# One more projection by seven half-size products, its input sums one group sooner, and three pieces of a decoder block's side work moved

## The chip, the cores and the metric

The kernel runs on one core of one Trainium2 chip. Its time is the device time of one execution in microseconds (us); a run's time is the median over executions. The engines are TensorE (PE, matrix products), VectorE (DVE), ScalarE (ACT), GpSimd (POOL), and SyncE (SP), which only issues transfers. Each takes its instructions in the order written.

## The reference

One layer of a decoder trunk, float32, 512 tokens, model width 1024:

```
h = RMSNorm(x);  h @ w_in -> GLA q, k, v, gate r, forget input
                             | attention q, k, v for 3 groups | two merge gates
A: gated linear attention, 4 heads, chunks of 64 (decay = exp of a running sum of log_sigmoid)
B: causal dilated attention, 3 groups x 4 heads, dilation 1, 4, 16; groups merged by softmax weight
x += (sigmoid(gA) * (A @ w_o_gla) + sigmoid(gB) * (B @ w_o_attn)) @ w_out
x += relu(RMSNorm(x) @ w_mlp1)^2 @ w_mlp2
x += sigmoid(RMSNorm(x) @ w_pg) * (p @ w_pp)
out = RMSNorm(x)
```

## The kernel before

Activations lie transposed (features on partitions, 512 tokens along the row). A product in float32 is made of three passes: each operand is split into a high part `hi` (rounded to fp32r, on ACT) and a rest `lo` (on DVE), and hi x hi, hi x lo, lo x hi are summed in PSUM. Weights come as units of 128 x 1024 (512 KB): `load` brings one to one of six raw buffers, and `fetch` makes its `hi` (line 226) and its `lo` (line 221). `weight` asks `fetch` to be two operands ahead of the one that PE is about to use. All matmuls of split products are recorded at line 240, in `run`.

There are two forms of a 1024 x 512 x 512 projection. The plain one (`fm`) is four units, each 24 matmuls with 512 columns. The other (`strassen`) takes 2 x 2 blocks of weights and inputs and does seven half-size products instead of eight, the rows of `STAGES`, each 24 matmuls with 256 columns. Its operands are blocks and sums of blocks of the weights: S1 and S3 are added up by an accumulating transfer that POOL issues (`prepare`, `sums`, lines 198 and 209), S2 and S4 by DVE (lines 206 and 212); the block A21 of a quad is loaded five operands early. The input sums T1 to T4 come from `xsums` and are split too. Results: a first product is copied from PSUM with ACT (line 312), and a later one is combined with it on DVE (line 330 or 332).

Everything else is side work, written as generators. `run` calls `step` after each eight matmuls; `step` takes one closure from the list `later` and, whenever `pace` columns have gone by, one piece of the first generator in `side`, which then goes back to second place (`WAYS` = 2). So two generators alternate, and a generator further down the list waits. `drain` runs all that is left without products between. The place of a piece in the program decides where it stands in each engine's queue.

The order: q0, k0 (group 0), a drain that ends with the normed input, then q1 and k1 (group 1, plain) with `scores0` and `xsums` as side work, a drain, q2 and k2 (seven products), v1 and v2 with `scores12`, v0, then gq, gk and gv0 with `pv` (attention output, one per head) and `decay` (the GLA decays, eight pieces with PE, then Exp, Ln and the scan on ACT and DVE), then the w_o_attn product with `gla` for two heads, the gates, w_o_gla, w_out, the MLP, w_pp, w_pg and the output. All intermediate 128 x 512 tiles come from one pool of `NU` tiles.

In the MLP, `rms_gen` makes 1/rms of the new x for each token: matmuls with ones, a power on POOL (`rsqrt`), a diagonal tile `dg`, its split, and two matmuls (lines 396, 397) that broadcast it. Each block of the hidden layer is `max(., 0) * rstd` (line 1167), then squared (line 1176). At the end, `evac_pg0` and `evac_pg1` take w_pg's result for 128 tokens: sigmoid (ACT, line 1267), two DVE operations, the square with its sum (ACT, line 1270), and then `scale_out` and `put` scale and store. The last 128 tokens are done in two halves of 256 columns.

Of the kernel before, what the change touches and what calls it, by code (L numbers as in the profile page):

```python
# [13 lines left out]
AF = mybir.ActivationFunctionType  # L14
OP = mybir.AluOpType
# [19 lines left out]
def att_col(g, which):  # L35
    return ATT + (g * 3 + which) * 512
# [5 lines left out]
def weight_units():  # L42

    u = []

    def fm(name, src, col, n, row=0):
        for j in range(n):
            u.append((f"{name}.{j}", "fm", src, row, col + j * P))

    def tm(name, src, col):  # L50
        for i in range(4):
            u.append((f"{name}.{i}", "tm", src, i * 2 * P, col))

    fm("q0", "w_in", att_col(0, 0), 4)
    u = u[NS:]
    def quad(name, src, col, kind="quad"):
        for m, k in ((0, 0), (1, 0), (1, 1), (0, 1)):
            u.append((f"{name}.A{m + 1}{k + 1}", kind, src, k, col + m * (P if kind == "quad" else 256)))

    fm("k0", "w_in", att_col(0, 1), 4)  # L60
    fm("q1", "w_in", att_col(1, 0), 4)
    fm("k1", "w_in", att_col(1, 1), 4)
    quad("q2", "w_in", att_col(2, 0))
    quad("k2", "w_in", att_col(2, 1))
    quad("v1", "w_in", att_col(1, 2), "quadt")
# [12 lines left out]
    for i in range(2):
        quad(f"ga{i}", "w_in", GATE + i * 512)
    fm("og", "w_o_gla", 0, 8)  # L80
    fm("wo", "w_out", 0, 8)
    for q in range(8):
        quad(f"m1q{q}", "w_mlp1", q * 512)
    for sub in range(2):
        for kk in range(16):
            u.append((f"m2s{sub}.{kk}", "tm", "w_mlp2", kk * 2 * P, sub * 512))
    for j in range(2):
        u.append((f"pp{j}.0", "tm", "w_pp", 0, j * 512))
    for j in range(2):
        tm(f"pg{j}", "w_pg", j * 512)  # L90
    return u
# [35 lines left out]
C_LN2, C_LN3, C_BA, C_GN, C_LN1, C_LO, C_N = 0, 8, 16, 20, 28, 36, 38  # L127
W0, W12 = 384, 256

NU, NW, PIECE, WAYS = 69, 5, 8, 2  # L130

NRAW = 6

NWARM = 8

# [2 lines left out]
def block_kernel(ctx, tc, xT, ws, pT, wts, wha, wa2, vec, lnf, rel, onehot, ident_d, mask_d, out):  # L138
# [231 lines left out]
        S.activation(t, x, AF.Square, scale=1.0 / 32.0)  # L370
        return t

    def rms_tok(acc):

        ps = smt()
        for i in range(4):
            TE.matmul(ps[:, i:i + 1], lhsT=acc[:, i * P:(i + 1) * P], rhs=ones[:, 0:1], start=True, stop=True)
        r = const.tile([P, 4], F32, name="rtok", bufs=3)
        rsqrt(r, ps[:, 0:4], 4)
        return r  # L380

    def rms_gen(acc, res, wait=0, gap=0):

        for _ in range(wait):
            yield
        r = rms_tok(acc[0])
        for _ in range(gap):
            yield
        dg = u32()
        V.tensor_tensor(dg.rearrange("p (a b) -> p a b", a=4), ident[:, None, :].to_broadcast([P, 4, P]),  # L390
                        r[:, :, None].to_broadcast([P, 4, P]), op=OP.mult)
        dh, dl = split(dg)
        for _ in range(2 + gap):
            yield
        pb = smt()
        TE.matmul(pb, lhsT=ones_r, rhs=dh, start=True, stop=False)
        TE.matmul(pb, lhsT=ones_r, rhs=dl, start=False, stop=True)
        bc = const.tile([P, T], F32, tag="rstd", name="rstd", bufs=2)
        S.activation(bc, pb, AF.Copy)
        res += [r, bc, pb]  # L400
# [81 lines left out]
        V.scalar_tensor_tensor(out=o, in0=a, scalar=-1.0, in1=b, op0=OP.mult, op1=OP.subtract)  # L482

    def xsums():
        for g in range(2):
            t1, t2, t3, t4 = (u32() for _ in range(4))
            for p in range(2):
                x0, x1 = (xn[4 * g + 2 * p + k][0] for k in range(2))
                o = halves(p)
                V.tensor_tensor(t1[:, o], x0[:, halves(0)], x0[:, halves(1)], op=OP.subtract)  # L490
                minus(t2[:, o], t1[:, o], x1[:, halves(1)])
                yield
                V.tensor_tensor(t3[:, o], x1[:, halves(1)], x0[:, halves(1)], op=OP.subtract)
                minus(t4[:, o], t2[:, o], x1[:, halves(0)])
                yield
            names, ts, hi = ("T1", "T2", "T3", "T4"), (t1, t2, t3, t4), [split_hi(t1)]
            for i in range(4):
                if i < 3:
                    hi.append(split_hi(ts[i + 1]))
                tx[names[i], g] = split_lo(ts[i], hi[i])  # L500
                yield

    def xs_op(name, pr):
        if name in ("B11", "B21", "B22"):
# [465 lines left out]
    q0 = [qk0_evac(p, HD_SCALE) for p in q0ps + [q0t]]  # L970
    k0 = [qk0_evac(fm(f"k0.{j}", xsr), 1.0) for j in range(4)]
    drain()
    side.append(scores0())
    side.append(xsums())
    q1 = qk_cls("q1", HD_SCALE)
    k1 = qk_cls("k1", 1.0)
    drain()
    q2 = heads("q2", HD_SCALE, True)
    k2 = heads("k2", 1.0, True)
    drain()  # L980
# [6 lines left out]
    side.append(weights())  # L987
    v0 = values("v0")
    drain()
    pace[0] = 2560  # L990
    side.extend(pv(h) for h in range(4))
    side.append(decay())
    gq = heads("gq", HD_SCALE)
    gk = heads("gk", 1.0)
    gv = [values("gv0", True)]
# [152 lines left out]
        later.extend(x1_tile(j))  # L1148
    while len(later) > 5:
        step()  # L1150
    side.append(rms_gen(acc1, norm2, 6, 2))


    hid = [None] * 32
# [4 lines left out]
    def quad(q):  # L1159


        def finish(m, t, s, ps):
            add(m, s, s, ps)

            def scale():
                o = s.rearrange("p (n t) -> p n t", n=2)
                V.scalar_tensor_tensor(out=o, in0=o, scalar=0.0,  # L1167
                                       in1=norm2[1][:, None, halves(t)].to_broadcast([P, 2, HT]),
                                       op0=OP.max, op1=OP.mult)

            def act():
                for n in range(2):
                    j = 4 * q + 2 * n + m
                    if hid[j] is None:
                        hid[j] = u32()
                    S.activation(hid[j][:, halves(t)], s[:, halves(n)], AF.Square)  # L1176

            later.extend([scale, act])

        def extra(i):  # L1180
            if i in (3, 4):
                later.append(lambda: hid_split(i - 3))

        strassen(f"m1q{q}", x1_op, finish, extra=extra if q == 7 else None)
# [6 lines left out]

    for q in range(8):
        quad(q)
        if q == 0 and not norm2:
            drain()
    for k in (2, 3):
        hid_split(k)
    drain()
# [2 lines left out]
    for sub in range(2):  # L1201
# [21 lines left out]
                    lnb.append(t)  # L1223
        for o in range(4):
            j = 4 * sub + o
            V.tensor_tensor(xx[j], xx[j], pss[o], op=OP.add)
            normed(j, C_LN3, x2s, acc2)
    while later:
        step()
# [30 lines left out]
    sp2 = const.tile([P, 4], F32, name="sp2")  # L1260
    fr = const.tile([P, 4], F32, name="fr")

    def gated(ps, i, c, tt, col):

        n = c.stop - c.start
        sg = u32()
        S.activation(sg[:, 0:n], ps[:, 0:n], AF.Sigmoid, scale=rt3[0][:, tt:tt + 1])
        V.tensor_tensor(sg[:, 0:n], sg[:, 0:n], pps[i][:, c], op=OP.mult)
        V.tensor_tensor(x2t[i][:, c], x2t[i][:, c], sg[:, 0:n], op=OP.add)
        S.activation(sg[:, 0:n], x2t[i][:, c], AF.Square, scale=1.0 / 32.0, accum_out=ss2[:, col:col + 1])  # L1270

    def evac_pg0(tt, ps):
        if len(x2t) < 8:
            drain()
        gated(ps, tt, slice(0, 512), tt, tt)
        V.tensor_scalar(sp2[:, tt:tt + 1], ss2[:, tt:tt + 1], EPS, None, op0=OP.add)
        V.tensor_tensor(x2t[tt], x2t[tt], lnb[0], op=OP.mult)

    def scale_out(tt, col):

        V.tensor_scalar(sp2[:, tt:tt + 1], ss2[:, col:col + 1], sp2[:, tt:tt + 1], None, op0=OP.add)
        GP.tensor_tensor(fr[:, tt:tt + 1], sp2[:, tt:tt + 1], mh[:, 0:1], op=OP.pow)
        o = u32()
        S.activation(o, x2t[tt], AF.Copy, scale=fr[:, tt:tt + 1])
        S.dma_start(out[tt * P:(tt + 1) * P, 0:512], o)

    def put(tt, c):
        n = c.stop - c.start
# [3 lines left out]
        SY.dma_start(out[tt * P:(tt + 1) * P, 512 + c.start:512 + c.stop], o[:, 0:n])  # L1292

    def evac_pg1(tt, ps):
        gated(ps, 4 + tt, slice(0, 512), tt, 4 + tt)
        scale_out(tt, 4 + tt)
        put(tt, slice(0, 512))

    tmaj("pg0", x2s, evac_pg0)
    tmaj("pg1", x2s, evac_pg1, tts=range(3))  # L1300
    tok = slice(3 * P, 4 * P)
    for f in range(2):
        c = slice(f * 256, (f + 1) * 256)
        ps = mmt()
        run(three(ps[:, 0:256], [(cols(x2s[k], tok), cols(ready[f"pg1.{k // 2}"], slice((k % 2) * 512 + c.start, (k % 2) * 512 + c.stop)))
                                 for k in range(KC)]))
        gated(ps, 7, c, 3, 8 + f)
        if f == 0:
            V.tensor_scalar(sp2[:, 3:4], ss2[:, 8:9], sp2[:, 3:4], None, op0=OP.add)
    scale_out(3, 9)  # L1310
    put(3, slice(256, 512))
    put(3, slice(0, 256))
# [85 lines left out]
```

## Time and profile before

| | |
|---|---|
| median of 3 runs | 990.1 us (989.91 to 991.78) |
| the profiled execution, its own time | 991.5 us |
| its span in the trace | 989.7 us |
| PE busy | 973.7 us (98%) |
| PE weight loads busy | 889.3 us (90%) |
| DVE busy | 689.4 us (70%) |
| ACT busy | 520.9 us (53%) |
| POOL busy | 94.4 us (10%) |

The profile is one execution. Busy shares say how much of the span an engine worked; matmuls are pipelined, so a busy PE is not PE at its peak. What ended an engine's idle time is inferred from its semaphores. Between the span and the time of the execution lie 1.8 us.

### The profile page before, as it was taken

Reading aid. Unit: us, or ns where it says so; the run is one execution under the profiler, and the core shown is the slowest. Engines: PE = TensorE matmul, PEld = TensorE weight load, DVE = VectorE, ACT = ScalarE, POOL = GpSimd, SP = SyncE. Lnnn points to the kernel's source line nnn. Section 1 sums busy time; section 2 is a strip of 40 time slices with the busy share of each in tenths; the row PEclk is TensorE's granted clock in tenths of the full one; section 3 lists DMA queues with packets and bytes.
Section 4 is the critical chain, followed back from the end, with each engine's and each line's share of the span. In section 5 each row is a group of like instructions: output and inputs, shape, how many; then the busy total and the mean of one; then the engine's idle time right before and its main releaser. Section 6 shows DMA issues by size and latency. Waiting matters only on the chain.

```text
span 989.7 us, 15873 instructions
## 1 busy us (share of the span) xinstructions
PE 973.7 (98%) x6372; PEld 889.3 (90%) x6372; DVE 689.4 (70%) x966; ACT 520.9 (53%) x875; POOL 94.4 (10%) x136
## 2 busy tenths in 40 slices
PE   9999999999998999999999999999999999999996
PEld 7788999999996999999988889999998888888885
DVE  7777579676579669977955697788778445653554
ACT  7335546445575667565733446555665335442633
POOL 0230011320010021013010001010000000000000
PEclk9999999999999999999999999999999999999999
DMA  8473564974264545455636426656544332523102
GB/s 308 126 205 100 128 147 112 266 202 115 80 157 131 160 98 149 121 146 171 171 92 206 126 46 164 177 131 169 154 145 131 104 96 77 167 88 106 43 1 85
DMA packets 40026, 133.63 MB, mean 135 GB/s; under 512 B 5203, under 2 KB 6815, under 8 KB 39952
## 3 DMA queue, kind: packets, MB, share of 16 engines
q1 hardware_dynamic: 27504, 92.51, 28.5%
q0 software_dynamic: 10720, 36.96, 18.4%
q10 hardware_dynamic: 1728, 3.15, 0.8%
q8 instruction: 50, 0.82, 0.3%
q14 instruction: 24, 0.20, 0.1%
HBM read 126.26 MB, written 8.17 MB: 136 GB/s over the span
## 4 chain that ended last, share of the span: by engine, by line
PE 92%; DVE 3%; issue 2%; ACT 1%; POOL 0%; POOLq 0%; DVEq 0%; ACTq 0%
PE mmt L240 73%; PE smt L240 9%; PE smt L829 1%; DVE lo L221 1%; PE smt L769 1%; PE smt L695 1%; PE mmt L454 1%; PE mmt L453 1%; PE mmt L455 1%; PE smt L875 1%; DVE u L818 0%; PE smt L877 0%; PE smt L428 0%; PE smt L665 0%; PE smt L786 0%
## 5 line engine op out<-in xcount | busy, mean ns | idle before, releaser
L240 PE MATMUL mmt<-ur,hi 128*128 128x256 f32 (+1 forms) x2784 | 608.5, 314 | 1.8 <-ACT u L1002 1.5
L240 PEld LDWEIGHTS mmt<-ur,hi 128*128 128x128 f32 x2784 | 459.9, 191 | 34.3 <-issue 1.9
L240 PE MATMUL mmt<-ur,lo 128*128 128x256 f32 (+1 forms) x1392 | 437.4, 314 | 0.5 <-DVE lo L221 0.5
L221 DVE TENSOR_TENSOR lo<-w,hi 128x1024 fp32r<-128x1024 f32 x236 | 286.2, 1220 | 119.6 <-PE mmt L240 64.2
L226 ACT ACTIVATE hi<-w 128x1024 fp32r<-128x1024 f32 x236 | 246.8, 1053 | 137.1 <-issue 64.0
L240 PEld LDWEIGHTS mmt<-ur,lo 128*128 128x128 f32 x1392 | 266.0, 191 | 16.3 <-DVE lo L221 0.7
L240 PE MATMUL mmt<-hi,ur 128*128 128x256 f32 (+1 forms) x736 | 154.5, 306 | 0.0
L337 ACT ACTIVATE ur<-u 128x512 fp32r<-128x512 f32 x136 | 79.9, 621 | 95.2 <-DVE u L1066 30.9
L240 PEld LDWEIGHTS mmt<-hi,ur 128*128 128x128 f32 x736 | 119.4, 191 | 5.6
L240 PE MATMUL mmt<-lo,ur 128*128 128x256 f32 (+1 forms) x368 | 112.4, 305 | 0.0
L345 DVE TENSOR_TENSOR ur<-u,ur 128x512 fp32r<-128x512 f32 x135 | 89.0, 686 | 20.3 <-ACT ur L337 19.7
L330 DVE TENSOR_TENSOR u<-u,mmt 128x512 f32<-128x512 f32 (+1 forms) x92 | 58.0, 654 | 39.0 <-PE mmt L240 37.4
L240 PE MATMUL smt<-ur,hi 128*128 128x512 f32 x272 | 83.7, 389 | 0.0
L312 ACT ACTIVATE u<-mmt 128x512 f32<-128x512 f32 x92 | 54.4, 592 | 49.7 <-PE mmt L240 49.7
L240 PEld LDWEIGHTS mmt<-lo,ur 128*128 128x128 f32 x368 | 70.2, 191 | 2.7
L240 PEld LDWEIGHTS smt<-ur,hi 128*128 128x128 f32 x272 | 51.1, 188 | 10.6
L240 PE MATMUL smt<-ur,lo 128*128 128x512 f32 x136 | 53.0, 390 | 0.0
L209 POOL DMA_DIRECT2D w<-in_wts_dram x23 | 20.1, 875 | 289.8 <-DVE w L206 210.5
L1176 ACT ACTIVATE u<-u 128x256 f32<-128x256 f32 x64 | 23.0, 409 | 37.2 <-DVE u L1167 37.2
L198 POOL DMA_DIRECT2D w<-in_wts_dram x23 | 20.4, 886 | 202.4 <-DMA w<-in_wts_dram 84.6
L240 PEld LDWEIGHTS smt<-ur,lo 128*128 128x128 f32 x136 | 25.5, 188 | 5.3
L212 DVE TENSOR_TENSOR w<-w 128x1024 f32<-128x1024 f32 x23 | 28.2, 1225 | 0.8
(203 smaller groups left out, 718.2 us busy)
## 6 DMA issues: line engine op xcount, KB each, us to landing
w<-in_wts_dram SPq DMA_DIRECT2D x167, 512.0 KB, 4.0
w<-in_wts_dram POOLq DMA_DIRECT2D x46, 512.0 KB, 5.5
u<-in_xT_dram SPq DMA_DIRECT2D x8, 256.0 KB, 4.7
v_dram<-u POOLq DMA_DIRECT2D x8, 256.0 KB, 6.2
u<-v_dram POOLq DMA_DIRECT2D x8, 256.0 KB, 7.3
y_dram<-u ACTq DMA_DIRECT2D x8, 256.0 KB, 2.4
u<-y_dram POOLq DMA_DIRECT2D x8, 256.0 KB, 7.3
u<-in_xT_dram POOLq DMA_DIRECT2D x8, 256.0 KB, 8.1
```

What stands on the lines that cost most here:

```text
L198: GP.dma_start(w, wts[UNIT[f"{q}.A22"]], accum_op=OP.add)
L209: GP.dma_start(w, wts[UNIT[f"{q}.A21"]], accum_op=OP.add)
L212: V.tensor_tensor(w, w, raw[f"{q}.A12"], op=OP.add)
L221: V.tensor_tensor(lo, w, hi.bitcast(F32), op=OP.subtract)
L226: S.activation(hi, w, AF.Copy)
L240: TE.matmul(o, lhsT=l, rhs=r, start=a, stop=b, skip_group_check=shared)
L312: S.activation(sums[c], bank[b], AF.Copy, scale=-scale if c[0] else scale)
L330: V.tensor_tensor(out, s, ps, op=OP.subtract if m else OP.add)
L337: S.activation(hi, x, AF.Copy)
L345: V.tensor_tensor(lo, x, hi.bitcast(F32), op=OP.subtract)
L453: TE.matmul(q0ps[i], lhsT=hi[:, c], rhs=xh, start=k == 0, stop=False)
L1176: S.activation(hid[j][:, halves(t)], s[:, halves(n)], AF.Square)
```

## The change

- Group 1's keys k1 are one more quad of seven products; `OPERANDS`, `EARLY` and the transfers follow from the list.
- `xsums` takes both halves of the input at once and makes T1, T4, T2, T3 in this order, all eight sum tiles at the start. It is put into `side` ahead of q1, and `scores0` only behind q1; the drain between k1 and q2 goes.
- `decay` stands in `side` ahead of the last head's `pv`, and `pace` stays at 2048 there.
- The MLP's norm is applied behind the second product: the hidden layer is `max(., 0)` squared, and the result is multiplied with 1/(mean square + eps) for each token, as the norm's factor is positive. `rms_gen` waits 30 steps instead of 6, with 4 instead of 2 between its parts, and uses a reciprocal on DVE.
- The last 128 tokens are done in 384 and 128 columns, with the squares behind both gates. The outputs of the first three token tiles are issued by SP instead of ACT.
- `NU` goes from 69 to 73, and the store for POOL's transfer descriptors is set to 8192 bytes.

```
-    fm("k1", "w_in", att_col(1, 1), 4)
+    quad("k1", "w_in", att_col(1, 1))
...
-NU, NW, PIECE, WAYS = 69, 5, 8, 2
+NU, NW, PIECE, WAYS = 73, 5, 8, 2
+LAST = 384
...
-    def rms_tok(acc):
+    def rms_tok(acc, squared=False):
...
-        rsqrt(r, ps[:, 0:4], 4)
+        if squared:
+            V.tensor_scalar(r, ps[:, 0:4], EPS, None, op0=OP.add)
+            V.reciprocal(r, r)
+        else:
+            rsqrt(r, ps[:, 0:4], 4)
...
     def xsums():
...
+        t1, t2, t3, t4 = ([u32(), u32()] for _ in range(4))
+        def x(g, p, k, t):
+            return xn[4 * g + 2 * p + k][0][:, halves(t)]
+        def sums(f):
+            for g in range(2):
+                for p in range(2):
+                    f(g, p, halves(p))
                 yield
+        def splits(name, ts):
+            his = [split_hi(ts[0]), split_hi(ts[1])]
+            yield
+            for g in range(2):
+                tx[name, g] = split_lo(ts[g], his[g])
+            yield
+        yield from sums(lambda g, p, o: V.tensor_tensor(t1[g][:, o], x(g, p, 0, 0), x(g, p, 0, 1), op=OP.subtract))
+        yield from splits("T1", t1)
+        yield from sums(lambda g, p, o: minus(t2[g][:, o], t1[g][:, o], x(g, p, 1, 1)))
+        yield from sums(lambda g, p, o: minus(t4[g][:, o], t2[g][:, o], x(g, p, 1, 0)))
+        yield from splits("T4", t4)
+        yield from splits("T2", t2)
+        yield from sums(lambda g, p, o: V.tensor_tensor(t3[g][:, o], x(g, p, 1, 1), x(g, p, 0, 1), op=OP.subtract))
+        yield from splits("T3", t3)
...
-    side.append(scores0())
     side.append(xsums())
     q1 = qk_cls("q1", HD_SCALE)
-    k1 = qk_cls("k1", 1.0)
-    drain()
+    side.append(scores0())
+    k1 = heads("k1", 1.0, True)
     q2 = heads("q2", HD_SCALE, True)
...
-    pace[0] = 2560
-    side.extend(pv(h) for h in range(4))
-    side.append(decay())
+    side.extend([pv(0), pv(1), pv(2), decay(), pv(3)])
...
-    side.append(rms_gen(acc1, norm2, 6, 2))
+    side.append(rms_gen(acc1, norm2, 30, 4, True))
...
-                V.scalar_tensor_tensor(out=o, in0=o, scalar=0.0,
-                                       in1=norm2[1][:, None, halves(t)].to_broadcast([P, 2, HT]),
-                                       op0=OP.max, op1=OP.mult)
+                V.tensor_scalar(s, s, 0.0, None, op0=OP.max)
...
-        if q == 0 and not norm2:
-            drain()
...
-            V.tensor_tensor(xx[j], xx[j], pss[o], op=OP.add)
+            t = u32()
+            V.tensor_tensor(t, pss[o], norm2[1], op=OP.mult)
+            V.tensor_tensor(xx[j], xx[j], t, op=OP.add)
...
-        S.dma_start(out[tt * P:(tt + 1) * P, 0:512], o)
+        (S if tt == 3 else SY).dma_start(out[tt * P:(tt + 1) * P, 0:512], o)
...
+    parts, sgs = [slice(0, LAST), slice(LAST, 512)], []
+    for c in parts:
+        ps, n = mmt(), c.stop - c.start
+        run(three(ps[:, 0:n], ...))
+        sgs.append(gate(ps, n, 3))
+        if c.start == 0:
+            gated(sgs[0], 7, c)
+    squares(sgs[0], 7, parts[0], 8)
+    gated(sgs[1], 7, parts[1])
+    V.tensor_scalar(sp2[:, 3:4], ss2[:, 8:9], sp2[:, 3:4], None, op0=OP.add)
+    squares(sgs[1], 7, parts[1], 9)
...
-    nc = _bacc.Bacc("TRN2", target_bir_lowering=False, num_devices=1)
+    nc = _bacc.Bacc("TRN2", target_bir_lowering=False, num_devices=1, dynamic_dma_scratch_size=8192)
```

## Rows read from the trace of the kernel before

**Rows 1.** Stretch: length; busy PE, PEld, DVE, ACT, POOL (instructions); clock; DMA share, GB/s.

```profile
150.00:175.00 25.00, 25.00 (x215) 25.00 (x214) 23.25 (x29) 16.94 (x43) 5.45 (x8) 1.00 0.45 116
300.00:325.00 25.00, 20.75 (x101) 15.75 (x100) 21.57 (x41) 15.81 (x28) 1.90 (x3) 1.00 0.41 118
575.00:600.00 25.00, 22.69 (x151) 20.93 (x150) 22.07 (x31) 13.62 (x21) 2.79 (x3) 0.94 0.39 86
```

**Rows 2.** PE's waits: who was waited for, us in total, times, longest.

```profile
PE smt L869 <- DVE u L857: 2.4, 2, 1.6
PE smt L396 <- ACT ur L337: 1.6, 1, 1.6
PE mmt L240 <- ACT u L1002: 1.5, 1, 1.5
...
PE mmt L240 <- DVE lo L221: 0.5, 1, 0.5
PE mmt L240 <- DVE u L330: 0.3, 1, 0.3
PE smt L397 <- DVE ur L345: 0.2, 1, 0.2
```

**Rows 3.** DVE in order of time: start, length, idle before with its end.

```profile
302.64 1.22 DVE L818 TENSOR_TENSOR_SCAN u<-u 128x512 f32<-128x512 f32 x1
...
312.46 0.29 DVE L857 COPY u<-u 128x256 f32<-128x256 f32 x1
```

**Rows 4.** DVE in order of time, at the MLP norm.

```profile
594.77 0.69 DVE L390 TENSOR_TENSOR u<-ident,rtok 128x512 f32<-128x512 f32 x1 [1.16 <-POOL rtok L365]
```

**Rows 5.** Busy time and granted clock behind the MLP norm's broadcast.

```profile
596.00:602.00 6.00, 5.54 (x29) 5.13 (x30) 5.08 (x6) 4.48 (x7) 0.00 (x0) 0.72 0.92 254
```

**Rows 6.** ACT in order of time: evacuations of k1 (L584) and q2 (L312).

```profile
94.66 0.60 ACT L584 ACTIVATE u<-mmt 128x512 f32<-128x512 f32 x1 [2.95 <-PE mmt L240]
100.10 0.60 ACT L584 ACTIVATE u<-mmt 128x512 f32<-128x512 f32 x1 [3.89 <-PE mmt L240]
111.29 0.60 ACT L312 ACTIVATE u<-mmt 128x512 f32<-128x512 f32 x1 [0.54 <-PE mmt L240]
114.17 0.60 ACT L312 ACTIVATE u<-mmt 128x512 f32<-128x512 f32 x1 [1.33 <-PE mmt L240]
```

**Rows 7.** Groups by line and shape: count | busy us, mean ns | idle before, releasers.

```profile
L221 DVE TENSOR_TENSOR lo<-w,hi 128x1024 fp32r<-128x1024 f32 x236 | 286.2, 1220 | 119.6 <-PE mmt L240 64.2 <-PE smt L240 31.2 <-ACT hi L226 24.0
L226 ACT ACTIVATE hi<-w 128x1024 fp32r<-128x1024 f32 x236 | 246.8, 1053 | 137.1 <-issue 64.0 <-DVE w L212 23.5 <-PE smt L240 23.3
L645 DVE TENSOR_TENSOR u<-smt,u 128x512 f32<-128x512 f32 x12 | 8.2, 687 | 1.6 <-PE smt L695 1.4 <-PE smt L666 0.2
L646 DVE TENSOR_REDUCE st<-u 128x2 f32<-128x512 f32 x12 | 8.2, 686 | 0.4
L332 DVE SCALAR_TENSOR_TENSOR u<-mmt,u 128x256 f32<-128x256 f32 x16 | 7.5, 516 | 6.8 <-PE mmt L240 6.7
```

**Rows 8.** The chain that ended last, in order of time: one group of `scores0`.

```profile
70.57 0.86 PE smt L695 x4
```

**Rows 9.** DVE in order of time, behind the second MLP product.

```profile
930.82 1.22 DVE L221 TENSOR_TENSOR lo<-w,hi 128x1024 fp32r<-128x1024 f32 x1 [2.04 <-ACT hi L226]
```

**Rows 10.** PE, ACT and DVE in order of time, at the end.

```profile
980.11 0.37 ACTq L1285 DMA_DIRECT2D out_dram<-u  x1
...
981.00 0.28 PE L240 MATMUL mmt<-hi,ur 128*128 128x256 f32 x1
...
982.37 0.46 ACT L1267 ACTIVATE u<-mmt,rtok 128x256 f32<-128x256 f32 x1
...
984.32 0.21 DVE L1281 TENSOR_SCALAR sp<-ss,sp 128x1 f32<-128x1 f32 x1 [0.58 <-ACT u L1270]
```

**Rows 11.** The chain that ended last: narrow float32 matmuls (L775 128 columns, L377 one column).

```profile
230.85 0.22 PE smt L775 x2
...
931.90 0.79 PE smt L377 x8
```

More of the change, by code (lines that the diff above doesn't have):

```diff
@@ L378, in rms_tok, with rms_gen @@
         r = const.tile([P, 4], F32, name="rtok", bufs=3)
-        rsqrt(r, ps[:, 0:4], 4)
+        if squared:
[3 more added lines that the diff above has]
+            rsqrt(r, ps[:, 0:4], 4)
         return r
-    def rms_gen(acc, res, wait=0, gap=0):
+    def rms_gen(acc, res, wait=0, gap=0, squared=False):
         for _ in range(wait):
             yield
-        r = rms_tok(acc[0])
+        r = rms_tok(acc[0], squared)
         for _ in range(gap):
@@ L484, in xsums @@
     def xsums():
[L485 to L491, printed above, removed]
-                yield
[L493 to L501, printed above, removed]
+        t1, t2, t3, t4 = ([u32(), u32()] for _ in range(4))
[5 more added lines that the diff above has]
+                    f(g, p, halves(p))
+                yield
+        def splits(name, ts):
[12 more added lines that the diff above has]
+        yield from splits("T3", t3)
     def xs_op(name, pr):
@@ L1163, in finish, with positive @@
             add(m, s, s, ps)
-            def scale():
-                o = s.rearrange("p (n t) -> p n t", n=2)
-                V.scalar_tensor_tensor(out=o, in0=o, scalar=0.0,
-                                       in1=norm2[1][:, None, halves(t)].to_broadcast([P, 2, HT]),
-                                       op0=OP.max, op1=OP.mult)
+            def positive():
+                V.tensor_scalar(s, s, 0.0, None, op0=OP.max)
             def act():
@@ L1176, in act @@
                     S.activation(hid[j][:, halves(t)], s[:, halves(n)], AF.Square)
-            later.extend([scale, act])
+            later.extend([positive, act])
         def extra(i):
@@ L1261, in block_kernel, with gate, gated, squares @@
     fr = const.tile([P, 4], F32, name="fr")
-    def gated(ps, i, c, tt, col):
-        n = c.stop - c.start
+    def gate(ps, n, tt):
         sg = u32()
         S.activation(sg[:, 0:n], ps[:, 0:n], AF.Sigmoid, scale=rt3[0][:, tt:tt + 1])
+        return sg
+    def gated(sg, i, c):
+        n = c.stop - c.start
         V.tensor_tensor(sg[:, 0:n], sg[:, 0:n], pps[i][:, c], op=OP.mult)
         V.tensor_tensor(x2t[i][:, c], x2t[i][:, c], sg[:, 0:n], op=OP.add)
+    def squares(sg, i, c, col):
+        n = c.stop - c.start
         S.activation(sg[:, 0:n], x2t[i][:, c], AF.Square, scale=1.0 / 32.0, accum_out=ss2[:, col:col + 1])
+    def gated_all(ps, i, tt, col):
+        sg = gate(ps, 512, tt)
+        gated(sg, i, slice(0, 512))
+        squares(sg, i, slice(0, 512), col)
     def evac_pg0(tt, ps):
@@ L1274, in evac_pg0 @@
             drain()
-        gated(ps, tt, slice(0, 512), tt, tt)
+        gated_all(ps, tt, tt, tt)
         V.tensor_scalar(sp2[:, tt:tt + 1], ss2[:, tt:tt + 1], EPS, None, op0=OP.add)
@@ L1294, in evac_pg1 @@
     def evac_pg1(tt, ps):
-        gated(ps, 4 + tt, slice(0, 512), tt, 4 + tt)
+        gated_all(ps, 4 + tt, tt, 4 + tt)
         scale_out(tt, 4 + tt)
@@ L1301, in block_kernel @@
     tok = slice(3 * P, 4 * P)
[L1302 to L1309, printed above, removed]
+    parts, sgs = [slice(0, LAST), slice(LAST, 512)], []
+    for c in parts:
+        ps, n = mmt(), c.stop - c.start
+        run(three(ps[:, 0:n], [(cols(x2s[k], tok), cols(ready[f"pg1.{k // 2}"], slice((k % 2) * 512 + c.start, (k % 2) * 512 + c.stop)))
+                               for k in range(KC)]))
+        sgs.append(gate(ps, n, 3))
[5 more added lines that the diff above has]
+    squares(sgs[1], 7, parts[1], 9)
     scale_out(3, 9)
```

## The prediction, made before the change was run

> **What bounds the kernel now.** I read the busy time by stretches first. TensorE (PE) is busy for 973.7 of the span's 989.7 us. A stretch like 150 to 175 is the rule, with all 25.00 us busy; 300 to 325 (20.75) and 575 to 600 (22.69) fall short [rows 1], and behind PE's last matmul stands a tail. So a change pays only if it gives PE fewer columns, fills one of these holes, or shortens the tail; time taken from VectorE (DVE), ScalarE (ACT) or a queue is worth nothing by itself.
>
> Next the list of PE's own waits [rows 2], which names who ended each hole. The reader is to see that it is short: 2.4 us on the copy at L857, 1.5 on the copy at L1002 and 0.3 on L330 (4.2 together, all in 300 to 325), then 1.6 on L337, 0.2 on L345 and 0.5 on L221 (2.3, the hole in 575 to 600). Then the timeline behind each wait, to see why the named engine was late.
>
> First hole: the last scan of `decay` ends on DVE at 303.9 [rows 3], while PE has already begun the w_o_attn products, whose side work is `gla`. `gla` needs that scan, so its copy L857, for which PE's transposes wait, runs only at 312.46. Second hole: the rms sum of the MLP norm goes to GpSimd (POOL) for the power, and DVE, idle for 1.16 us, gets the result at 594.77 [rows 4]; then ACT and DVE split it, and PE's broadcast matmuls stand in PE's order in front of the next products. Behind that wait of 1.6 us the granted clock is 0.72 on the mean of 596 to 602 [rows 5]: between the two levels (1.2 and 2.4 GHz), so the lower one for part of it.
>
> **Second group's keys.** Four products of 24 matmuls with 512 columns become seven of 24 with 256. The evacuations of two products of a kind in a row give the pitch: 100.10 - 94.66 = 5.44 us for the wide, 114.17 - 111.29 = 2.88 us for the half-size one [rows 6]. 4 x 5.44 = 21.76 against 7 x 2.88 = 20.16: 1.6 us less, on PE, which sets the end there. The transposed-order copies on ACT go (four), four scaled copies on ACT and eight combinations of 0.516 us on DVE [rows 7] come, with three more hi/lo splits (1.053 on ACT, 1.220 on DVE each) and two weight sums on DVE of about the same 1.22.
>
> Whether DVE can feed this: k1 asks of DVE 7 x 1.22 + 2 x 1.22 + 8 x 0.516 = 15.1 us, and since `scores0` is now queued behind q1, its eight softmax steps fall into k1, 8 x (0.687 + 0.686) = 11.0 us [rows 7], and with the last quarter of `xsums` (four half-width sums and two lo halves, at most 6 x 0.69 = 4.1) 29 to 30 us. PE has 20.2 us of products there and the eight groups of score matmuls, at most 0.86 each [rows 8], so 26 to 27 us. DVE ends some 3 to 4 us behind, but `fetch` makes each operand two products (5.8 us) before its use, and q2 carries no side work, so the debt is paid there. The same mixture stands in the trace: in 150 to 175 DVE is busy 23.25 of 25.00 us with scores12 beside v1 and PE loses nothing [rows 1]. I price it at nothing; if the lead is used up, one to two products' worth is lost, 0 to 3 us. `xsums` itself only moves into q1, where DVE then has six of the eight lo halves and three quarters of the sums in 21.8 us. The early A21 load for k1 is issued with the first weights, its accumulating A22 stands on POOL in front of the first norm; six raw buffers hold both, and POOL has nothing else there. Its cost is nothing unless the load comes late.
>
> **Decay ahead of pv(3), pace back to 2048.** The three quads gq, gk, gv0 give 63 steps. At pace 2560 four of five steps serve the side list, about 50, and the list has 4 x 8 + 21 = 53 pieces, so the last scans fell into the drain. At 2048 each step serves: piece 53 stands at step 53, ten steps of a third of 2.88 us (9.6 us) before gv0 ends. `decay`'s last scan then ends near 288 instead of 303.9, `gla` starts when gv0's last splits are done, and L857 comes about 8 us sooner while PE waited 1.6 us at most. So all 4.2 us go; the bounds are 0 (the lateness only moves to another piece of `gla`) and 4.2. pv(3) now ends near step 48, before its product needs `oa`; its PE work is the same.
>
> **MLP norm late.** The rms sum is taken 30 steps after the start instead of 6, with a reciprocal on DVE in place of POOL's power; 6 steps (5.8 us) lie between the split and the broadcast, where 4 (3.8) did before. That removes 1.6 + 0.2 us of waiting and with it the half clock: (1 - 0.72) x 6 us = 1.7 us. Together 3.5. Bounds: 1.8, if another pause lowers the clock, and 4.0, if the 0.5 on L221 goes too. POOL's queue loses the power that stood between two accumulating loads. The hidden tiles lose a multiplication and keep a maximum on DVE, off the path. At the end of each half of the second MLP product four multiplications of about 0.69 are added; behind the last half they delay DVE by 2.7 us, but DVE's idle 2.04 us in front of 930.82 [rows 9] and the eight w_pp products of PE, 6 x 0.227 = 1.4 us each, which need none of it, take this. Without that cover it would be 2.7.
>
> **The tail.** Before, PE does the last tile in halves of 256 columns, 24 matmuls of 0.12 each, and ends at 981.28 [rows 10], so it began at 981.28 - 5.76 = 975.5; ACT reaches the first gate only behind the output issue of tile 2 (980.11, 0.37 us), though PE ended that half near 978.4, and the second gate stands behind the first half's square, at 982.37. From there to the last norm sum, 984.32, are 1.95 us: gate, two DVE steps, square, sum. After: the issue goes to SP, and ACT is free at 980.1. 384 columns cost, on the line through 512 (5.44 / 24 = 0.227) and 256 (2.88 / 24 = 0.120), 0.173, so 4.16 us, ready near 979.7; their gate and DVE steps are over before the narrow part is. The 128-column part has no row. Its ends: the same line, 0.067 x 24 = 1.6 us; and 5.3, if these columns cost what a float32 product of 128 does, two matmuls with 0.22 together [rows 11]. Nearest is the weight load, which eight matmuls of one column show, 0.79 / 8 = 0.099 [rows 11]: I take 2.4. So the second gate stands at 975.5 + 4.16 + 2.4 = 982.1, and the chain behind it is shorter by 128 columns in each of four steps, 0.1 to 0.17 each (a quarter of the 0.687 for 512 is the upper end), but has the first part's square in it beside the DVE steps, so about 1.5: 983.6, 0.7 us gained. With 1.6 for the part the same working gives 1.5 gained, with 5.3 a loss of 2.2.
>
> On that part the Trainium skill (TensorE: Matmul & The Clock Gate, "Back-to-back issue gap") gives a sustained pitch of load and matmul of about 81 ns at 128 columns and 131 at 512. By it the part would take 1.9 us and the sum would be some 0.4 us lower. The rows here do not agree at 512 columns (227 ns), so I leave it aside.
>
> Four more tiles and a smaller descriptor store for POOL's transfers: no wait of PE comes from either [rows 2]; nothing.
>
> **Sum.** 1.6 + 4.2 + 3.5 + 0.7 = 10.0. The profiled execution: span 989.7 to 979.7, its time 991.5 to 981.5. It lies 1.4 above the median of the three runs, so the median goes from 990.1 to 980.1.
>
> **Rivals.**
> A, the forecast, 978.3 to 981.8: 0.50.
> B, the `gla` wait stays in part: pv(3) and `decay` now share the last steps of gv0, and ACT still has its exponentials and table load there. Half of 4.2 stays: 982.2, up to 984.3. For it: ACT took part in the wait (1.5 on L1002). Against: ten steps of margin. 0.13.
> C, the narrow part of the tail runs at the float32 price: 980.1 + 2.9 = 983.0. For it: no split product here is narrower than 256. Against: nothing in the rows says that they change price. 0.17.
> D, DVE falls behind in k1: 3 us of waiting, and if it comes in one piece the clock again (1.7): 983.1 to 984.8. Against: DVE in 150 to 175 [rows 1]. 0.05.
> E, slower than before: the tile pool. `xsums` takes its eight sum tiles at once and makes the sixteen split tiles while q0, k0 and the normed x are alive. If the new quad's tiles must wait for these, the hi and lo of a product no longer run ahead: 1.05 + 1.22 = 2.27 us for each of the seven products of k1, 15.9: 996. It decides from five products on (10.0 / 2.27 = 4.4). Against: the pool grows by four, and no hole is ended by a wait for a tile [rows 2]. 0.05.
> F, the change does not do what it says: the two holes move with their work (`gla` behind gv0's last splits, the broadcast behind DVE's backlog) and only 1.6 + 0.7 stay: 987.8, give or take 0.8. 0.10.
>
> About 0.2%, 2 us, is what a measurement of this kernel can tell from no change. A to D and half of F are faster by more: 0.90. Half of F within it: 0.05. E: 0.05. The range 978.3 to 984.7 holds A, B, C and most of D, over 0.8; F and E are left out.
>
> **What would show it.** k1's products at a pitch of 2.88 with no PE wait on L221 or a hi tile; no PE wait on L857 or L1002 behind gv0; no wait at the MLP norm's broadcast and the clock at 1.00 from 575 to 625; transposes and w_pg products behind the MLP without a wait; the pitch of the 128-column matmuls in the tail, and the last norm sum about 0.7 us nearer to PE's start of the last tile (8.8 us behind it before). What makes it wrong: a PE wait on DVE's lo tiles or on `xsums` in k1 or q2, a pitch over 0.2 in the last 24 matmuls, or the half clock in a new place.

## The result, and the profile after

| | before | after |
|---|---|---|
| median | 990.9 us (4 runs, 989.91 to 994.52) | 981.0 us (4 runs, 980.75 to 982.6) |
| profiled execution, its time | 991.5 us | 981.07 us |
| its span | 989.7 us | 979.3 us |
| PE busy | 973.7 us (98%) | 970.4 us (99%) |
| DVE busy | 689.4 us (70%) | 695.4 us (71%) |

The ratio of the times is 0.9897, 95% interval 0.9869 to 0.9925: 1.0% less time, with the whole interval below 1. The 981.0 us lie inside the range given, 0.9 us above the value given.

PE's list of waits after the change, to be read beside [rows 2] (lines after the change stand 2 to 21 higher, L221 is now L223):

```profile
PE smt L434 <- POOL ones L429: 1.0, 1, 1.0
PE mmt L242 <- DVE lo L223: 0.8, 2, 0.5
```

The first is the start of the kernel (L428 before). Of the holes of [rows 2] only the lo tile is left, now with two waits. The windows of the changed kernel (length; busy us of PE, PEld, DVE, ACT, POOL with counts; granted clock, DMA share, GB/s), first k1's seven products, then three stretches that the prediction spoke of, then two stages from the first matmul of one to the first of the next:

```profile
77.40:103.60 26.20, 26.20 (x202) 25.56 (x201) 23.75 (x41) 19.77 (x47) 1.48 (x2) 1.00 0.39 101
...
300.00:325.00 25.00, 25.00 (x138) 20.93 (x137) 18.80 (x38) 16.27 (x31) 1.91 (x3) 1.00 0.58 176
575.00:600.00 25.00, 24.17 (x197) 23.59 (x197) 24.71 (x33) 17.09 (x27) 1.74 (x2) 1.00 0.62 157
600.00:625.00 25.00, 25.00 (x210) 24.91 (x208) 18.33 (x23) 15.65 (x26) 2.60 (x3) 1.00 0.55 139
...
294.17:323.17 29.00, 29.00 (x148) 23.94 (x147) 23.59 (x45) 18.95 (x34) 2.77 (x4) 1.00 0.58 163
573.37:737.56 164.19, 163.36 (x1356) 162.69 (x1355) 125.84 (x153) 100.18 (x161) 11.31 (x13) 1.00 0.58 154
```

The same two stages of the kernel before:

```profile
295.92:330.17 34.25, 30.00 (x149) 23.62 (x147) 30.24 (x52) 18.48 (x34) 1.90 (x3) 1.00 0.47 133
580.38:747.59 167.21, 164.90 (x1356) 164.08 (x1354) 132.75 (x152) 99.48 (x161) 12.10 (x14) 0.99 0.58 151
```

Against [rows 1], 300 to 325 is full (25.00 for 20.75), 575 to 600 nearly (24.17 for 22.69), with the clock at 1.00. The two pairs of stages give the price of each hole directly: 34.25 to 29.00, and 167.21 to 164.19 (the last with the half clock of this execution, and with 0.83 us of waits left).

Three timelines of the changed kernel (start, length, engine, line, operation; in brackets the idle time before it and what ended it), DVE first, with the counterparts of [rows 3] and of the last norm sum in [rows 10], then PE with the norm's broadcast and the last 128 columns, then the gate behind these on ACT:

```profile
287.29 1.22 DVE L834 TENSOR_TENSOR_SCAN u<-u 128x512 f32<-128x512 f32 x1
...
305.08 0.29 DVE L873 COPY u<-u 128x256 f32<-128x256 f32 x1
...
973.87 0.21 DVE L1302 TENSOR_SCALAR sp<-ss,sp 128x1 f32<-128x1 f32 x1 [0.34 <-ACT u L1286]
```

```profile
615.18 0.40 PE L402 MATMUL smt<-ur,ones_r 128*128 128x512 f32 x1
...
969.38 0.39 PE L242 MATMUL mmt<-hi,ur 128*128 128x384 f32 x2
969.61 0.27 PE L242 MATMUL mmt<-lo,ur 128*128 128x128 f32 x1
969.72 0.39 PE L242 MATMUL mmt<-hi,ur 128*128 128x128 f32 x2
969.95 0.28 PE L242 MATMUL mmt<-lo,ur 128*128 128x128 f32 x1
...
972.07 0.28 PE L242 MATMUL mmt<-hi,ur 128*128 128x128 f32 x1
```

```profile
972.38 0.37 ACT L1275 ACTIVATE u<-mmt,rtok 128x128 f32<-128x128 f32 x1 [1.82 <-PE mmt L242]
```

The copy comes 7.4 us sooner than its counterpart in [rows 3] (1.75 of it because the whole stage starts sooner), and no idle time stands in front of the broadcast. (A row with x2 joins two matmuls of one kind under the shape of the first: the row at 969.38 is the last of 384 columns and the first of 128.)

PE's timeline cut at every change of shape (plain or half-size products, weights or tokens as the moving operand) shows where each microsecond went. Lengths in us, from the start of the first matmul listed with the new shape to the next one; the last row goes to the end of the span. The columns after the second are the experiments below.

| stage | before | after | k1_alone | norm_alone | pace_only | order_only | norm_early | nu69 | sums_late |
|---|---|---|---|---|---|---|---|---|---|
| up to k0 | 29.08 | 29.27 | 29.01 | 29.54 | 29.28 | 29.24 | 29.08 | 29.32 | 29.56 |
| k0, q1, k1, q2, k2 | 116.57 | 114.63 | 114.62 | 116.57 | 114.63 | 114.63 | 114.63 | 114.63 | 118.33 |
| v1 to gv0 | 150.27 | 150.27 | 150.26 | 150.28 | 150.33 | 150.62 | 150.31 | 150.31 | 150.31 |
| w_o_attn | 34.25 | 29.00 | 33.87 | 35.58 | 29.01 | 34.45 | 29.00 | 29.01 | 29.01 |
| gates to w_o_gla | 163.14 | 163.14 | 163.13 | 163.15 | 163.13 | 163.15 | 163.14 | 164.47 | 163.13 |
| MLP, first product | 167.21 | 164.19 | 167.15 | 164.17 | 164.17 | 164.18 | 164.73 | 164.18 | 164.17 |
| MLP, second, to last tile | 227.89 | 227.98 | 227.89 | 227.93 | 227.98 | 227.98 | 227.94 | 227.98 | 227.98 |
| last tile to the end | 14.22 | 13.76 | 14.20 | 14.21 | 13.70 | 13.78 | 13.70 | 13.74 | 13.74 |
| span | 989.7 | 979.3 | 987.2 | 988.5 | 979.3 | 985.1 | 979.6 | 980.7 | 983.3 |

The missing stage, w_out, is 87.1 in all. So the change is 0.19 - 1.94 - 5.25 - 3.02 + 0.09 - 0.46, with 0.01 in w_out: 10.4 us of span. (Joined rows make the last tile start 0.1 to 0.2 late in this list; by single matmuls the last two terms are +0.04 and -0.47.) The first term is no part of the change: the stage up to k0 waits for the input's transfers and lies between 29.0 and 29.7 in all traces here. To read the medians, one has to know that of 16 executions of the kernel before whose clock is known, nine had a mean granted clock of 0.997 or 0.998 and spans of 987.9 to 989.6 us, while seven, the profiled one (989.7) among them, had 0.995 or 0.996 and 989.5 to 990.9.

### The profile page after: what moved, and what is told of

Same layout as the page of the kernel before. It is cut to its first block, busy times and chain, and to the rows that moved or that the text cites. A ratio compares the mean times of both kernels' runs of the same rounds, so it can differ in the third digit from the quotient of the medians.

```text
span 979.3 us, 16042 instructions
## 1 busy us (share of the span) xinstructions
PE 970.4 (99%) x6444; PEld 891.5 (91%) x6444; DVE 695.4 (71%) x988; ACT 525.7 (54%) x878; POOL 96.8 (10%) x137
## 4 chain that ended last, share of the span: by engine, by line
PE 96%; DVE 2%; issue 1%; DMA 0%; ACT 0%; SPq 0%; POOLq 0%; POOL 0%; DVEq 0%
PE mmt L242 77%; PE smt L242 9%; PE smt L845 1%; PE smt L785 1%; PE smt L711 1%; PE smt L891 1%; PE mmt L460 1%; PE mmt L461 0%; DVE lo L223 0%; PE mmt L459 0%; DMA u<-in_xT_dram 0%; PE smt L893 0%; DVE ur L347 0%; PE smt L682 0%; PE smt L801 0%
## 5 line engine op out<-in xcount | busy, mean ns | idle before, releaser
L223 DVE TENSOR_TENSOR lo<-w,hi 128x1024 fp32r<-128x1024 f32 x239 | 290.2, 1220 | 112.5 <-PE mmt L242 65.9
L228 ACT ACTIVATE hi<-w 128x1024 fp32r<-128x1024 f32 x239 | 250.1, 1054 | 129.9 <-issue 77.6
L242 PEld LDWEIGHTS mmt<-ur,lo 128*128 128x128 f32 x1416 | 269.3, 190 | 15.6 <-DVE lo L223 1.2
L242 PE MATMUL mmt<-hi,ur 128*128 128x256 f32 (+3 forms) x736 | 156.4, 308 | 0.0
L242 PE MATMUL mmt<-lo,ur 128*128 128x256 f32 (+3 forms) x368 | 112.7, 306 | 0.0
L314 ACT ACTIVATE u<-mmt 128x512 f32<-128x512 f32 x96 | 56.8, 592 | 59.5 <-PE mmt L242 59.4
L332 DVE TENSOR_TENSOR u<-u,mmt 128x512 f32<-128x512 f32 (+1 forms) x100 | 62.3, 651 | 34.1 <-PE mmt L242 33.9
L211 POOL DMA_DIRECT2D w<-in_wts_dram x24 | 21.4, 891 | 281.0 <-DVE w L208 172.9
L200 POOL DMA_DIRECT2D w<-in_wts_dram x24 | 21.7, 904 | 242.4 <-DVE lo L223 68.5
```

Source lines behind the costliest of these rows:

```text
L200: GP.dma_start(w, wts[UNIT[f"{q}.A22"]], accum_op=OP.add)
L211: GP.dma_start(w, wts[UNIT[f"{q}.A21"]], accum_op=OP.add)
L223: V.tensor_tensor(lo, w, hi.bitcast(F32), op=OP.subtract)
L228: S.activation(hi, w, AF.Copy)
L242: TE.matmul(o, lhsT=l, rhs=r, start=a, stop=b, skip_group_check=shared)
L314: S.activation(sums[c], bank[b], AF.Copy, scale=-scale if c[0] else scale)
```

## The experiments

**Keys by seven products alone**, put into the kernel before with the new `xsums` and the smaller descriptor store (`k1_alone`):

```
-    fm("k1", "w_in", att_col(1, 1), 4)
+    quad("k1", "w_in", att_col(1, 1))
...
-NU, NW, PIECE, WAYS = 69, 5, 8, 2
+NU, NW, PIECE, WAYS = 73, 5, 8, 2
...
-    side.append(scores0())
     side.append(xsums())
     q1 = qk_cls("q1", HD_SCALE)
-    k1 = qk_cls("k1", 1.0)
-    drain()
+    side.append(scores0())
+    k1 = heads("k1", 1.0, True)
     q2 = heads("q2", HD_SCALE, True)
...
-    nc = _bacc.Bacc("TRN2", target_bir_lowering=False, num_devices=1)
+    nc = _bacc.Bacc("TRN2", target_bir_lowering=False, num_devices=1, dynamic_dma_scratch_size=8192)
```

> The kernel before with only group 1's keys as seven products, the input sums one group sooner, the four more tiles and the smaller descriptor store. Theory (PE's columns set this stage): 1.6 us less by the pitches, up to 2.0 as the changed kernel's trace has it between the start of q1 and the first attention output, so a span of 987.7 to 988.1; no PE wait on a lo tile between q1 and k2; the two holes of the kernel before (4.2 and 2.3 us of PE's waits, half clock behind the second) stand as they were, 1.6 to 2.0 us sooner. Rival 1: DVE or the tile pool falls behind, PE waits on lo tiles in k1, span 989 or more. Rival 2: the drains behind k2 take the gain back, span 989.5.

Measured: span 987.2, 0.5 below the lower end expected. The stage is 1.95 us shorter, as in the changed kernel, with no wait of PE in it. The hole in w_o_attn stays, but is 0.4 shorter in this execution (33.87), and the one in the MLP stays, half clock included:

```profile
595.00:600.00 5.00, 5.00 (x32) 5.00 (x31) 4.29 (x6) 3.04 (x6) 0.00 (x0) 0.69 1.00 286
```

So the parts don't lean on each other here, and both rivals fall.

**The late norm alone**, in the kernel before (`norm_alone`): `rms_tok`, `rms_gen`, the hidden tiles and the multiplication behind the second product as in the changed kernel, `rms_gen(acc1, norm2, 30, 4, True)`, and no drain behind the MLP's first quad; nothing else.

> The kernel before with only the MLP norm late. Theory (the wait at the broadcast and the half clock behind it are the whole gain): no wait at the broadcast, granted clock 1.00 from 575 to 625, span 3.5 to 4.0 us shorter, 985.7 to 986.2; the hole of 4.2 us behind gv0 stays. Rival 1: DVE's four more multiplications behind the MLP hold PE up there, 2.7 us given back, span 988.5. Rival 2: another pause in 575 to 600 still lowers the clock, 1.8 us gained, span 987.9.

Measured: span 988.5, outside the theory's range. It is the very number of rival 1, but not for that rival's reason, as the stages show. The MLP's first product is 164.17, 3.04 less, with no wait at the broadcast and the clock at 1.00, and the multiplications behind the second product cost nothing (227.93). The 3.04 are 0.5 below the lower end expected. But w_o_attn, where nothing was changed, took 35.58 instead of 34.25, since in this execution the clock fell behind its hole (window of `norm_alone`):

```profile
315.00:320.00 5.00, 4.46 (x17) 3.66 (x17) 4.97 (x11) 3.53 (x6) 0.00 (x0) 0.66 0.42 159
```

By the clock this would be (1 - 0.66) x 5 = 1.7 us. The stage is only 1.33 longer (35.58 against 34.25), with waits of the same 4.2 us, and in this window PE was idle for 0.54. The same hole, as long, left the clock at 1.00 in the profile before. So in these traces a hole costs its length, and in some executions the half clock on top of it: 1.3 us here.

**Steps or order?** Two variants of the changed kernel: the old order with the new pace (`pace_only`), and the new order with the old pace (`order_only`).

```
-    side.extend([pv(0), pv(1), pv(2), decay(), pv(3)])
+    side.extend([pv(0), pv(1), pv(2), pv(3), decay()])
```

> The changed kernel with decay behind the four heads' sums again, as before, at pace 2048. Theory (the number of steps decides: 53 pieces in 63 steps): the last scan some 4 to 5 steps later than the changed kernel's 287.3, about 292, still 5 us before the w_o_attn product; span within 0.3 us of 979.3. Rival (the order decides): PE waits for the first copy of gla again, 1 us or more, span 980.5 to 983.5.

```
+    pace[0] = 2560
     side.extend([pv(0), pv(1), pv(2), decay(), pv(3)])
```

> The changed kernel with pace 2560 in the gq, gk, gv0 products as before, decay ahead of the last head's sums. Theory (steps decide): some 50 pieces are served, the last pieces of the last head fall into the drain; gla has its scans in time, but the w_o_attn product then waits for the last head's output: a hole of 1 to 3 us, span 980.3 to 982.3. Rival (the order alone does it): no wait, span within 0.3 us of 979.3.

Measured: `pace_only` 979.3, w_o_attn 29.01, and the last scan was only 0.3 us later, not 4 to 5:

```profile
287.62 1.22 DVE L834 TENSOR_TENSOR_SCAN u<-u 128x512 f32<-128x512 f32 x1
```

`order_only` 985.1, w_o_attn 34.45, more than either expectation allowed: the old hole is back, with the same waiters as in [rows 2] (2.0 on the copy of `gla`, 1.2 on the evacuation), and behind it the half clock. A window and DVE's timeline of `order_only`:

```profile
310.00:315.00 5.00, 4.10 (x14) 2.98 (x15) 4.90 (x14) 3.79 (x6) 0.00 (x0) 0.67 0.69 256
```

```profile
297.90 1.23 DVE L834 TENSOR_TENSOR_SCAN u<-u 128x512 f32<-128x512 f32 x1
...
299.74 1.23 DVE L834 TENSOR_TENSOR_SCAN u<-u 128x512 f32<-128x512 f32 x1
...
310.56 0.29 DVE L873 COPY u<-u 128x256 f32<-128x256 f32 x1
```

So the pace alone does all of it. The clock cost at most (1 - 0.67) x 5 = 1.65; without it the order alone would have 32.8 or a little more, so it is worth 1.4 at most. At 2560 the last pieces of `decay` still fall into the drain, though `pv(3)` stands behind it: the two alternate, and my theory that only the last head's sums would be late was wrong.

**The early norm** in the changed kernel (`norm_early`):

```
-    side.append(rms_gen(acc1, norm2, 30, 4, True))
+    side.append(rms_gen(acc1, norm2, 6, 2, True))
```

> The changed kernel with the norm's sum taken 6 steps after the start of the MLP and 2 steps between its parts, as before, but with the reciprocal on DVE and the norm still applied behind the second product. Theory (the place of the sum and the broadcast in PE's order is what was gained): PE waits for the broadcast again, for 0.6 to 1.0 us since POOL's power of 1.05 us is gone, or for lo tiles that the norm's four DVE steps push back; first MLP product 165.0 to 165.5 us instead of 164.2, and up to 1.7 us more where the half clock follows: span 980.1 to 982. Rival (taking the multiplication out of the hidden tiles' path is what was gained): no new wait, span within 0.3 us of 979.3.

Measured: span 979.6, and the stage is 164.73, 0.54 more, with the broadcast waiting again (PE's timeline):

```profile
588.11 0.50 PE L402 MATMUL smt<-ur,ones_r 128*128 128x512 f32 x1 [0.60 <-ACT ur L339]
588.83 0.50 PE L403 MATMUL smt<-ur,ones_r 128*128 128x512 f32 x1 [0.22 <-DVE ur L347]
```

The clock stayed at 1.00 behind it. Median 981.64 us of 4 runs (980.95 to 983.41), ratio to before 0.9908 (0.9891 to 0.9926). So the place in PE's order is worth 0.5 us, less than the 0.8 to 1.3 expected. The other 2.48 of the 3.02 lie between the kernel before and this one, which have the same three waits. Listed waits make 0.97 of it (2.31 against 1.34, nearly all at the broadcast, 0.60 for 1.56), and PE's busy time 1.51 (164.90 against 164.73 - 1.34 = 163.39 for the same matmuls): that is what the half clock of the profiled execution cost, a little less than the 1.7 by [rows 5]. That the shorter wait is owed to the reciprocal in place of POOL's power is likely, but no run shows it alone.

**Tiles and descriptor store.** The changed kernel with both as before (`pool_as_before`), and with the 69 tiles alone, the first two lines (`nu69`):

```
-NU, NW, PIECE, WAYS = 73, 5, 8, 2
+NU, NW, PIECE, WAYS = 69, 5, 8, 2
...
-    nc = _bacc.Bacc("TRN2", target_bir_lowering=False, num_devices=1, dynamic_dma_scratch_size=8192)
+    nc = _bacc.Bacc("TRN2", target_bir_lowering=False, num_devices=1)
```

> The changed kernel with 69 tiles in the pool and the default descriptor store, as before. Theory (no wait of PE comes from either): span within 0.3 us of 979.3. Rival (the eight sum tiles taken at once need the four tiles): PE waits on lo tiles or sums in q1 or k1, 1 us or more, up to the 15.9 us that the prediction worked out for all seven products.

> The changed kernel with 69 tiles in the pool, but with the smaller descriptor store. The run with both as before lost 1.3 us in the w_o_gla stage (370.97 to 486.31 there), where ACT waited 4.7 us for a split tile. Theory (the number of tiles is what was missing): the same wait of PE, about 1.1 us listed, and a stage of about 116.7 us. Rival (the descriptor store, by way of POOL's transfers): no such wait, a stage of 115.3 us.

Measured: 980.7 us both. The first fits neither its theory nor the place that the rival gave; the second settles which of the two edits it is. The loss of 1.33 us is in gates to w_o_gla, far behind the new products. PE's waits and ACT's timeline of `nu69`:

```profile
PE smt L845 <- DVE ur L924: 1.1, 1, 1.1
```

```profile
425.72 0.42 ACT L921 ACTIVATE ur<-u 128x256 fp32r<-128x256 f32 x1 [4.72 <-PE smt L845]
```

ACT stands 4.72 us before it may write a split tile of `gla`, until PE has read an older one; in the changed kernel three of these copies follow one another from 420.09 without such a wait. So the four tiles are part of the change, and the store, which changed nothing at 69 tiles, is not.

**The input sums where they were** (`sums_late`): the changed kernel with the old `xsums`, queued behind `scores0` ahead of q1, and a drain in front of k1.

```
...
-    side.append(xsums())
-    q1 = qk_cls("q1", HD_SCALE)
     side.append(scores0())
+    side.append(xsums())
+    q1 = qk_cls("q1", HD_SCALE)
+    drain()
     k1 = heads("k1", 1.0, True)
```

> The changed kernel with the input sums as before: made half by half, queued behind the group 0 scores, and drained between q1 and k1, since k1 by seven products needs them. Theory (the twelve steps of q1 serve only half of the list, and what is left runs with no product beside it): a hole of PE of 8 to 12 us in front of k1, the half clock behind it (about 1.7 us), and k1 to v1 some 6 us shorter since the scores are out of it: span 984 to 989, so most of the whole change's gain is gone. Rival (q1 has room for all): no hole, span within 0.5 us of 979.3.

Measured: span 983.3, 0.7 below the range expected. There are three waits in k1, 2.7 us together, and no half clock (PE's timeline):

```profile
89.31 0.38 PE L242 MATMUL mmt<-ur,hi 128*128 128x256 f32 x1 [0.86 <-ACT ur L339]
...
90.38 0.38 PE L242 MATMUL mmt<-ur,hi 128*128 128x256 f32 x1 [0.69 <-DVE ur L347]
...
93.31 0.39 PE L242 MATMUL mmt<-ur,lo 128*128 128x256 f32 x1 [1.12 <-DVE lo L223]
```

The stage takes 118.33: 3.7 more than with the sums one group sooner, and 1.8 more than with four plain products. So the seven products pay only when their sums are ready in time.

**The last tile in 256 and 256 columns**, the rest of the tail as in the changed kernel (`last256`, then `last256_again` timed beside `after_again`, the changed kernel itself):

```
-LAST = 384
+LAST = 256
```

> The changed kernel with the last tile in two parts of 256 columns instead of 384 and 128. Theory (a pass of 128 columns costs PE nearly as much as one of 256, 0.111 against 0.120 us): PE ends at 965.54 + 48 x 0.12 = 971.3 instead of 972.35; the chain behind it is some 0.2 to 0.3 us longer (256 columns instead of 128 in each step); last norm sum 0.7 to 0.9 us sooner, span 978.4 to 978.6. Rival (the short chain behind 128 columns is what the split buys): the last norm sum no sooner, span 979.3 or more.

> The changed kernel once more, beside the version with 256 and 256 columns at the end. Theory: stages as in its first trace within 0.1 us, start apart; median 980.9 to 981.2.

> The changed kernel with the last tile in 256 and 256 columns, timed beside the changed kernel itself. Theory: last tile to end 13.18 us against 13.76, so a median 0.5 to 0.6 us below that of the changed kernel. Rival: the 0.6 us of the first look was the one execution, medians within 0.2 us.

The gate of the second part on ACT and the last norm sum on DVE in `last256`, to be read beside the changed kernel's above:

```profile
971.46 0.47 ACT L1275 ACTIVATE u<-mmt,rtok 128x256 f32<-128x256 f32 x1 [0.87 <-PE mmt L242]
```

```profile
973.42 0.21 DVE L1302 TENSOR_SCALAR sp<-ss,sp 128x1 f32<-128x1 f32 x1 [0.45 <-ACT u L1286]
```

`last256` has span 978.8, a little above the 978.4 to 978.6 expected, and median 980.42 of 4 runs (980.12 to 980.94). In the changed kernel three matmuls of 128 columns take 0.34 us (969.61 to 969.95), 0.11 each, where 256 columns take 0.12 [rows 6]: PE saves almost nothing on the narrow ones. With halves the gate comes 0.92 sooner, the chain behind it is 1.96 instead of 1.49, and from the last tile to the end it is 13.18 and 13.19 us in its two traces, against 13.76 and 13.70 for the changed kernel. Timed side by side: `last256_again` 980.96 (980.35 to 982.05) and `after_again` 981.34 (980.6 to 981.76, a little above the expectation), ratios to before 0.9898 (0.9880 to 0.9915) and 0.9899 (0.9884 to 0.9913). The half microsecond is in the traces; the medians can't show it. Read against the kernel before, whose last tile was also cut in halves, the traces say more: from 14.22 to 13.18, so the issue moved to SP and the squares behind both gates bring 1.0 us, and the cut at 384 gives 0.6 of it back. No run separates the issue from the squares.

**The wait that is left** (`fetch_early`): the third MLP operand is prepared in front of the last pieces of the new x.

```
+    fetch(OPERAND["wo.7"] + NW - 2)
     while len(later) > 5:
```

> The changed kernel with the third MLP operand's hi and lo tiles made in front of the last pieces of the new x instead of behind them. Theory (the two waits of 0.53 and 0.3 us are for a lo tile that stands behind these pieces on DVE): both waits go, first MLP product 0.8 to 1.2 us shorter, span 978.1 to 978.5. Rival (DVE has no room there): the pieces come 1.2 us later and PE waits for one of their split tiles instead, span 979.0 to 980.5.

Measured: 979.0, but the MLP's first product is 164.09, only 0.1 less. One lo wait went, and PE waits for an evacuation on ACT instead:

```profile
582.64 0.50 PE L242 MATMUL mmt<-ur,hi 128*128 128x256 f32 x2 [0.69 <-ACT u L314]
...
586.32 0.39 PE L242 MATMUL mmt<-ur,lo 128*128 128x256 f32 x1 [0.30 <-DVE lo L223]
```

That span is smaller than the changed kernel's because its start was 0.24 sooner. DVE, busy for 24.70 of the 25.00 us from 575 (24.71 in the changed kernel), has no room for a reordering. The rival holds in its time; the wait that it named, on a split tile, is not the one that came.

## Why the prediction was right, point by point

**Keys by seven products: 1.6 forecast, 1.94 measured.** The pitches held. 12 products of 5.44 and 14 of 2.88 leave 10.97 of the old stage for side work, 8 and 21 leave 10.63 of the new one: the side matmuls cost 0.34 less among the half-size products, which I had not counted and whose cause no run isolates. DVE was not behind: k1's stretch, 77.40 to 103.60, has it busy for 23.75 us, not 29 to 30. All of the score work is there, but only four of the eight combinations, and 2.1 us of `xsums` instead of 4.1. Rival D had no footing. Rival E was wrong in its place, not in its kind: the pool does bind, but in `gla`, and for 1.33 us.

**Decay and pace: 4.2 forecast, 5.25 measured.** The mechanism is the one given: steps enough for all pieces, no wait on the copy, which comes at 305.08 instead of 312.46 [rows 3]. Three corrections. The last scan ended at 288.5, near the 288 forecast, but partly by luck: the stage that needs it starts 1.75 sooner, so the lead is 5.7 us, where 7.9 were forecast. The order, which I worked out together with the pace, adds nothing to it (`pace_only`). Rivals B and F are out: no wait of `gla` is left. And the size is wrong at one step: I took the sum of PE's listed waits for the price of the hole and set 4.2 as its upper bound. The stage lost 1.05 more, of which 1.00 stands in the windows as busy time, 30.00 against 29.00 for the same matmuls. A listed wait begins at the end of the last matmul, 0.39 us after its start at 512 columns, where the next would have followed after 0.227; and the first matmul behind a wait is longer (0.50 for L402 in `norm_early`, 0.40 for the same one in the changed kernel). Together 0.26 for each of four waits. `nu69` has as much, 1.07 us idle and 1.33 lost; `norm_early` has not, 0.5 more listed and 0.54 lost, so it is no fixed toll, and its cause is argued, not shown. The Trainium skill (TensorE: Matmul & The Clock Gate, "Single matmul latency") gives a single bf16 matmul a fixed part of some 0.17 us at the full clock beside its columns. The rows have 0.39 - 0.227 = 0.163 for it, but the ends of matmuls are modelled in the profile, so this is no measurement of its own.

**MLP norm late: 3.5 forecast, 3.02 measured.** No wait at the broadcast, clock 1.00 from 575 to 625, four multiplications without effect: all as given. Two things made it smaller. The 0.5 on L221, which the 3.5 did not count on, stayed, but a second wait of 0.3 joined it (0.8 in two), so the waits fell by 1.48 and not by 1.8. And the half clock had cost 1.5 and not 1.7. It was still the largest term (1.5, then 0.97 for the shorter wait, and 0.54 for the place in PE's order).

**Tail: 0.7 forecast, 0.46 measured.** The 384 columns took 4.18 us (0.174 each), as on my line. The 128 took 24 x 0.11 = 2.6, not 2.4, and the gate follows 0.2 us behind PE, which I had left out; the chain behind it was 1.49, as given. The narrow cut itself, for which I worked out the shorter chain, was a loss: with 256 and 256 columns the last norm sum comes 0.6 us sooner after the start of the tile (`last256`), and what gained is the rest of the edit. Rival C is out (0.22 each). The rule of the Trainium skill that I set aside ("Back-to-back issue gap", 81 ns at 128 columns) does not hold here: 110 ns.

**The sum.** 10.0 forecast, 10.4 in the two profiled spans, 9.9 in the medians, which agrees for a worse reason than it seems. The step that was wrong is the last: I took the whole sum from the median. But the half clock of the profiled execution was 1.7 of it (1.5 as measured), and by their times (990.1 and 989.91, 1.8 above the span) two of the three runs behind the median of 990.1 did not have it. Without the clock the stages give 1.94 + 5.25 + 1.5 + 0.4 = 9.1, from 988.1 us, a usual span of the nine, to 979.0, where the changed kernel's runs lie (979.0 to 979.3, one at 980.8). The forecast's own terms without the clock were 8.3. They were 1.4 too small for k1 and decay and 0.6 too large for the norm's waits and the tail, which hid about half of the 1.7 that did not belong there: that 980.1 came within 0.9 us of 981.0 is in part luck. The 9.9 rests besides on a median of the kernel before (990.9) that a fourth run of 994.52 moved up.

## What to carry to other kernels

Price a hole by the length of its stage with and without it, from traces cut at the same matmuls, and not by the sum of the waits listed in it, which was a fifth too small for the largest hole here. Before a profile's sum is taken from a median, look at what the profiled execution had that others may lack, such as the clock behind a hole. Where side work is served by a counter of columns, count pieces against steps first: here the pace alone moved the whole 5.25 us.

## What was not expected of the hardware

- The granted clock fell behind the hole in w_o_attn in two traces (0.66 in `norm_alone`, 0.67 in `order_only`) and stayed at 1.00 in two others with waits as long (before, `k1_alone`). It cost less than its share of the window: 1.33 us where (1 - 0.66) x 5 is 1.7.
- A load and matmul pair of the split products takes 0.227 us at 512 columns, 0.174 at 384, 0.120 at 256 and 0.110 at 128: from 256 to 128 columns next to nothing is gained.
- With four tiles fewer, a kernel whose new tiles are needed at 60 to 100 us loses 1.33 us at 425.
